# Streaming encoder step on one core: edges of order between prepared work and recurrence work on VectorE, ScalarE and GpSimd

## The chip, the cores and the metric

The kernel runs on one NeuronCore of a Trainium2 chip. The metric is the device time of one execution, in microseconds; of several executions the median is given.

## The reference

One layer of a hybrid streaming encoder over a prompt of 2048 positions and eight sample sequences of 16 positions each, all in float32, model width 1024:

```python
h = rms_norm(x, norm_mix)
p = h @ w_in                      # 3880 columns: q, k, v, z, gates of GDN; r, k, v, decay, gates of RWKV-7
x = x + concat(GDN(p_gdn), RWKV7(p_rwkv)) @ w_out
up = rms_norm(x, norm_ffn) @ w_up # 2 x 2816 columns
x = x + (silu(conv3(up[:, :2816])) * up[:, 2816:]) @ w_down
y = rms_norm(x, norm_final)
```

GDN is a gated delta rule with four heads of 128; RWKV-7 has eight heads of 64. Both carry a state from position to position. The q, k, v columns pass a short causal convolution of width 4, the RWKV columns one of width 2, the gate of the FFN one of width 3. Outputs are y and the final states of both request groups.

## The kernel before, in words

**Groups and phases.** The 16 blocks of 128 prompt positions are cut into five groups of 3, 4, 3, 3, 3 blocks; the last group carries the 128 sample positions too. A group's tiles are 128 channels by 384 or 512 positions. Each group has an input phase (`phase_in`, L551) and an output phase (`phase_out`, L1182). Their order is in0, in1, in2, out0, in3, out1, in4, out2, out3, out4 (`order`, L1293).

**Projections.** A product in float32 is made of three products of split operands: hi times hi, hi times lo, lo times hi (`mm3`, L447). A weight tile is split by `split_w` (L433): ScalarE casts the high part (L439), and VectorE or GpSimd in turn subtract it (L443). An activation tile is split by `split_x` (L507): ScalarE makes the high part (L512 or L515), VectorE the low part (L513 or L516). A phase splits its eight tiles of x first and then runs the blocks of columns, each into one of four PSUM banks. In an input phase the squares of x are summed beside the splits (`sumsq`, L477, L484). In an output phase the splits of `og` come first, then after `w_out` the splits of the new residual `res`.

**Prepared work.** The results of a column block are evicted, convolved (`conv`, L520: the history copy L526 on GpSimd, the eviction L527 on VectorE, the last tap L529 on ScalarE, the other taps L531 on VectorE), gated and stored to DRAM for the recurrences (`prep_gdn`, `prep_rwkv`, `l2scale`). In an output phase the same helpers make the FFN's gate, and L1241 adds a product in PSUM to the residual.

**Recurrence work.** `gdn_block` (L859) and `rwkv_half` (L1016) load a block's prepared tensors, build a 128 by 128 triangular system, invert it by seven doubling levels (`inverse`, L796: product pR, mask L821, product pX, addition L839), and advance the state. They run as tasks between the pieces of a later group's projection. Their many small steps go back and forth between TensorE and VectorE, ScalarE and GpSimd.

**Order of the work.** Everything is emitted by Python generators. `drive` (L391) holds a planner's clock of TensorE time (`mm` adds the cost of each product) and steps whichever task is due. Tasks have a rank: the projections, their prepared work and the norms have 0, the tails of the recurrences 1, RWKV 2, GDN 3. All that one step of a generator emits stands together. TensorE executes in the order of emission (`manual_schedule` names its engine, L1272). The order on VectorE, ScalarE, GpSimd and SP is set at compile time by the scheduler of the language, which takes, on its own estimate of time, the operations that are ready, so an operation emitted later may stand ahead of one emitted sooner on the same engine. Each engine then executes its list in order. All DMAs are issued from SP. Two places tie an operation behind the last one emitted on VectorE by hand (`behind`, L428, used at L653 and L781).

## Time and profile before

| | |
|---|---|
| median of three executions | 3531.19 us (3529.71 to 3534.89) |
| the profiled execution | 3535.21 us |
| its span, first to last instruction | 3533.4 us |
| mean granted clock of TensorE | 0.978 |
| TensorE busy with products | 3355.5 us (95%) |
| VectorE, GpSimd, ScalarE busy | 2371.1, 1843.7, 1512.1 us |

A row of a group or of the timeline gives the line, the engine (PE is TensorE, PEld its weight loads, DVE VectorE, ACT ScalarE, POOL GpSimd, SP the DMA queue), the operation, and what it writes and reads by the program's names. A row of waits says which engine's line waited for which other: total us, times, longest. A square bracket in the timeline gives the idle time of the engine before the operation and what ended it. Times are in us from the start of the span.

### The profile page before, as it was taken

Reading aid. Unit: us, or ns where it says so; the run is one execution under the profiler, and the core shown is the slowest. Engines: PE = TensorE matmul, PEld = TensorE weight load, DVE = VectorE, ACT = ScalarE, POOL = GpSimd, SP = SyncE. Lnnn points to the kernel's source line nnn. Section 1 sums busy time; section 2 is a strip of 40 time slices with the busy share of each in tenths; the row PEclk is TensorE's granted clock in tenths of the full one; section 3 lists DMA queues with packets and bytes.
Section 4 is the critical chain, followed back from the end, with each engine's and each line's share of the span. In section 5 each row is a group of like instructions: output and inputs, shape, how many; then the busy total and the mean of one; then the engine's idle time right before and its main releaser. Section 6 shows DMA issues by size and latency. Waiting matters only on the chain. (4 is left out here: it accounts for less than half of the span.)

```text
span 3533.4 us, 60005 instructions
## 1 busy us (share of the span) xinstructions
PE 3355.5 (95%) x21661; PEld 2888.1 (82%) x21661; DVE 2371.1 (67%) x4277; ACT 1512.1 (43%) x2698; POOL 1843.7 (52%) x2335
## 2 busy tenths in 40 slices
PE   8979989999999989999999999899999999999997
PEld 7857778889999878778877667699988899988886
DVE  6777777787666776766565777676657665665444
ACT  5554444444333454443333545443333444453333
POOL 4546556556666545556444445466656355534442
PEclk9989999999999999999999999999999999999999
DMA  5544444453333444533233334533334533443332
GB/s 170 170 127 135 144 151 126 131 174 113 115 114 105 123 145 148 173 93 91 90 93 90 121 120 144 186 116 113 114 119 153 164 120 126 138 143 96 96 94 82
DMA packets 346265, 447.58 MB, mean 127 GB/s; under 512 B 30168, under 2 KB 194336, under 8 KB 345968
## 3 DMA queue, kind: packets, MB, share of 16 engines
q1 hardware_dynamic: 345968, 443.75, 40.5%
q8 instruction: 170, 2.79, 0.3%
q14 instruction: 127, 1.04, 0.1%
HBM read 372.60 MB, written 71.03 MB: 126 GB/s over the span
## 5 line engine op out<-in xcount | busy, mean ns | idle before, releaser
L439 ACT CAST whi<-w 128x512 fp32r<-128x512 f32 (+1 forms) x1070 | 651.4, 610 | 1101.9 <-PE psd L362 282.8
L443 POOL TENSOR_TENSOR wlo<-w,whi 128x512 fp32r<-128x512 f32 (+1 forms) x535 | 705.0, 1318 | 721.9 <-ACT whi L439 695.1
L362 PE MATMUL psi<-x,whi 128*128 128x384 f32 (+1 forms) x2480 | 730.9, 376 | 34.5 <-ACT x L515 16.1
L362 PEld LDWEIGHTS psi<-x,whi 128*128 128x128 f32 x2480 | 454.1, 194 | 96.1 <-issue 21.6
L362 PE MATMUL psga<-x,whi 128*128 128x384 f32 (+1 forms) x1760 | 502.4, 366 | 0.0
L362 PE MATMUL psup<-x,whi 128*128 128x384 f32 (+1 forms) x1760 | 497.1, 363 | 0.0
L443 DVE TENSOR_TENSOR wlo<-w,whi 128x512 fp32r<-128x512 f32 (+1 forms) x535 | 428.2, 800 | 79.5 <-ACT whi L439 78.9
L362 PE MATMUL psi<-x,wlo 128*128 128x384 f32 (+1 forms) x1240 | 453.7, 366 | 4.3 <-POOL wlo L443 4.1
L362 PEld LDWEIGHTS psga<-x,whi 128*128 128x128 f32 x1760 | 318.5, 190 | 28.8 <-issue 3.6
L362 PEld LDWEIGHTS psup<-x,whi 128*128 128x128 f32 x1760 | 315.6, 188 | 26.6 <-issue 1.8
L362 PE MATMUL psd<-ah,whi 128*128 128x384 f32 (+1 forms) x880 | 328.1, 373 | 5.8 <-ACT ah L1231 5.8
L362 PE MATMUL psd<-al,whi 128*128 128x384 f32 (+1 forms) x880 | 318.8, 362 | 5.0 <-POOL al L1233 5.0
L362 PE MATMUL psd<-ah,wlo 128*128 128x384 f32 (+1 forms) x880 | 318.5, 362 | 0.0
L362 PE MATMUL psga<-x,wlo 128*128 128x384 f32 (+1 forms) x880 | 316.3, 359 | 0.0
L362 PE MATMUL psup<-x,wlo 128*128 128x384 f32 (+1 forms) x880 | 314.5, 357 | 0.0
L1241 DVE TENSOR_TENSOR res<-res,psd 128x384 f32<-128x384 f32 (+1 forms) x240 | 145.3, 606 | 201.3 <-PE psd L362 200.2
L362 PEld LDWEIGHTS psi<-x,wlo 128*128 128x128 f32 x1240 | 240.0, 194 | 28.0 <-POOL wlo L443 7.1
L1233 POOL TENSOR_TENSOR al<-xin,ah 128x384 fp32r<-128x384 f32 (+1 forms) x110 | 125.9, 1145 | 143.8 <-ACT ah L1231 103.1
L839 DVE TENSOR_TENSOR TUr<-TUr,pX 128x256 f16<-128x256 f16 x396 | 149.1, 413 | 73.4 <-PE pX L362 72.1
L527 DVE TENSOR_TENSOR P<-psga,rsx 128x384 f32<-128x384 f32 (+1 forms) x110 | 64.3, 585 | 192.9 <-PE psga L362 186.9
L362 PE MATMUL pso<-x,whi 128*128 128x384 f32 (+1 forms) x640 | 185.5, 370 | 2.1 <-DVE x L513 0.9
L362 PEld LDWEIGHTS psd<-ah,whi 128*128 128x128 f32 x880 | 166.6, 189 | 22.0 <-ACT ah L1231 7.2
(342 smaller groups left out, 6759.6 us busy)
## 6 DMA issues: line engine op xcount, KB each, us to landing
w<-in_w_up SPq DMA_DIRECT2D x440, 256.0 KB, 2.7
w<-in_w_in SPq DMA_DIRECT2D x310, 256.0 KB, 2.7
w<-in_w_down SPq DMA_DIRECT2D x160, 256.0 KB, 2.7
rX<-rx SPq DMA_DIRECT2D x68, 320.0 KB, 4.4
w<-in_w_out SPq DMA_DIRECT2D x80, 256.0 KB, 3.0
w<-in_w_down SPq DMA_DIRECT2D x80, 192.0 KB, 2.4
rx<-res SPq DMA_DIRECT2D x48, 192.0 KB, 3.0
gd<-res SPq DMA_DIRECT2D x48, 192.0 KB, 2.8
```

Of the source, the lines that this page charges most:

```text
L362: self.nc.tensor.matmul(out, lhsT=lhsT, rhs=rhs, start=start, stop=stop)
L439: nc.scalar.copy(hi, w)
L443: eng.tensor_tensor(lo, w, hi.bitcast(F32), SUB)
L527: nc.vector.tensor_tensor(P[:, h:h + g.P], ps[:, 0:g.P], rs[:, 0:g.P], MUL)
L839: nc.vector.tensor_tensor(w, w, pX[:, y].rearrange("p u (n b) -> p u n b", b=b), ADD)
L1233: nc.gpsimd.tensor_tensor(lo, y, hi.bitcast(F32), SUB)
L1241: nc.vector.tensor_tensor(res[m], res[m], ps, ADD)
```

## The change

The engines that the build writes to are wrapped. Each operation that is emitted on VectorE, ScalarE or GpSimd inside a step of a task with rank above 0 becomes that engine's mark. Each operation that is emitted outside such a step, and not inside `split_w`, gets an edge of order (no semaphore) to the mark of its own engine, so the scheduler may not put it ahead of it. Recurrence operations get no edge among themselves and none to prepared work; the splits of weights get none either. No instruction is added or removed, and the computation is the same.

```diff
+class Engine:
+    def __init__(self, b, eng):
+        self.b, self.eng, self.mark = b, eng, None
+
+    def __getattr__(self, op):
+        f = getattr(self.eng, op)
+
+        def run(*a, **k):
+            i = f(*a, **k)
+            if self.b.inrec:
+                self.mark = i.ins
+            elif self.mark is not None and not self.b.splitting:
+                self.b.tc.add_manual_dep(i.ins, self.mark.name, mybir.DependencyInfo(mybir.DependencyClass.NoSync, mybir.DependencyReason.DATA), reason="behind the recurrences")
+            return i
+        return run
+
+class Chip:
+    def __init__(self, b, nc):
+        self.nc = nc
+        self.vector, self.scalar, self.gpsimd = (Engine(b, e) for e in (nc.vector, nc.scalar, nc.gpsimd))
+
+    def __getattr__(self, name):
+        return getattr(self.nc, name)
...
-        self.tc, self.nc, self.I, self.O = tc, tc.nc, I, O
+        self.tc, self.nc, self.I, self.O = tc, Chip(self, tc.nc), I, O
+        self.inrec, self.splitting = False, False
...
     def step(self, task):
+        self.inrec = task[1] > 0
...
         out = []
+        self.splitting = True
         for w in ws or self.load_w(src, tiles):
...
             out.append((hi, lo))
+        self.splitting = False
         return out
```

## The prediction, made before the changed kernel was run

> **What bounds the kernel now.** I read the page first: its span, the busy line and the row of the GpSimd halves of the weights' splits.

> ```profile
> span 3533.4 us, 60005 instructions
> PE 3355.5 (95%) x21661; PEld 2888.1 (82%) x21661; DVE 2371.1 (67%) x4277; ACT 1512.1 (43%) x2698; POOL 1843.7 (52%) x2335
> L443 POOL TENSOR_TENSOR wlo<-w,whi 128x512 fp32r<-128x512 f32 (+1 forms) x535 | 705.0, 1318 | 721.9 <-ACT whi L439 695.1
> ```

> TensorE is the bound: 3533.4 - 3355.5 = 177.9 us of it are idle, and its order is written out, so an edge on another engine can only change how long it idles and how it is clocked. The change touches what VectorE, ScalarE and GpSimd run next, so the second view is who TensorE waits for.

> ```profile
> PE pA L362 <- DVE rA L1045: 18.2, 9, 4.5
> PE psi L362 <- ACT x L515: 16.1, 5, 7.1
> PE pR L362 <- DVE TUr L839: 12.3, 6, 5.6
> PE pX L362 <- DVE Rr L821: 8.1, 9, 2.5
> PE pSs L362 <- DVE gwm L988: 7.3, 4, 4.9
> ...
> PE pA L362 <- ACT rtok L1050: 6.0, 3, 2.3
> ...
> PE psi L362 <- DVE x L516: 5.3, 9, 1.6
> ...
> PE ptr L372 <- DVE TUg L839: 0.2, 1, 0.2
> ```

> Columns: total us, times, longest. The rows of this view whose releaser is a recurrence's tile (rA, TU, R, gwm, U, rtok and the like) are 25; the first and the last of them stand here, and they add up to 91.0 us, 2.6% of the span. That is all that shorter recurrence waits could ever return, apart from the clock.

> The third view, the timeline of VectorE at such waits, says what the late operation stood behind. Three kinds:

> ```profile
> 237.73 4.50 DVE L531 SCALAR_TENSOR_TENSOR res<-P,par,res 128x512 f32<-128x512 f32 x2
> 242.15 0.41 DVE L821 TENSOR_TENSOR Rr<-pR,msk 128x256 f16<-128x256 f32 x1
> 242.62 0.28 PE L362 MATMUL pX<-Rr,TUr 128*128 128x64 f16 x4 [1.37 <-DVE Rr L821]
> 1367.87 0.43 DVE L713 TENSOR_SCALAR lx<-lx 128x384 f32<-128x384 f32 x1 [1.15 <-POOL lx L712]
> 1368.33 0.96 DVE L714 TENSOR_TENSOR_SCAN ls<-scm,lx 128x387 f32<-128x387 f16 x1
> 1369.21 0.67 DVE L1045 TENSOR_TENSOR rA<-pA,msk 128x512 f32<-128x512 f32 x1
> 2284.10 0.69 DVE L443 TENSOR_TENSOR wlo<-w,whi 128x512 fp32r<-128x512 f32 x1 [1.89 <-ACT whi L439]
> 2284.70 1.28 DVE L1045 TENSOR_TENSOR rA<-pA,msk 128x512 f32<-128x512 f32 x2
> ```

> At 242 the mask `Rr` ran after two convolution taps of a column block that the code emits after it: this is what the change forbids. At 1368 `rA` stood behind decay work (L713, L714) that the code emits before `rA`: no edge touches that. At 2284 `rA` stood behind a split of weights, which the change sets aside. The longest single waits for `rA` and `gwm` in the rows above (4.5 and 4.9 us) are of the last two kinds or of the recurrence's own chain.

> **The change, part by part.** *What moves.* An edge ties each prepared operation to the last recurrence operation emitted on its engine (its mark), no more. I laid the order in which the code of before emits its operations beside the order in which the trace executes them. On VectorE 262 of 2052 prepared operations run before their mark, on ScalarE 85 of 1130, on GpSimd 146 of 972. Only these 493 are moved. 119 of GpSimd's are the tiny history copies of L526, which run long before their convolution, so their delay is hidden by that slack; I cost them at nothing (if the slack is gone, a copy is 0.4 us in front of a tap).

> *What it can return.* I followed each recurrence wait of TensorE back along its engine while that engine had no idle time. In 22 of the 70 that exceed 0.15 us a moved operation stands in this backlog; capping each by the smaller of wait and moved work gives 15.7 us. The first of the 22 is the one at 242, the last is this:

> ```profile
> 2802.61 0.70 PE L362 MATMUL pA<-rX 64*128 64x256 f32 x4 [2.31 <-ACT rtok L1050]
> 701.67 1.14 PE L362 MATMUL pKK<-gkq 128*128 128x256 f32 x2 [1.76 <-ACT gE L884]
> core 0: us, PE busy (x) PEld busy (x) DVE busy (x) ACT busy (x) POOL busy (x), PEclk, DMA share, GB/s
> 701.80:705.20 3.40, 3.40 (x9) 2.50 (x10) 0.00 (x0) 1.27 (x4) 3.40 (x4) 0.50 0.01 4
> ```

> The last two rows price the clock: a wait of 1.76 us is followed by 3.4 us at a granted clock of 0.50, which loses about half of 3.4, 1.7 us. Five of the 22 places (242 to 245, 1511 to 1513, 2029, 2570 to 2572, 2802) are followed by such a stretch: 5 x 1.7 = 8.5. So the most that can come back is 15.7 + 8.5 = 24.2 us. I take 60%, 14.5: a prepared operation that steps aside returns at once behind the mark and is in front of the next recurrence step.

> [...]

> *What it takes.* At the start of a projection the splits of x (L512 to L516) are emitted behind the recurrence step then open, and today they run ahead of it. Busy time of the VectorE splits alone, in the stretch that ends with the first product that reads them:

> ```profile
> 754.00:760.10 6.10, 2.42 (x5) 1.00 0.91 287
> 1211.00:1231.50 20.50, 4.33 (x5) 0.92 0.45 135
> 1985.00:2006.10 21.10, 4.61 (x5) 0.92 0.35 110
> 2726.00:2749.50 23.50, 5.30 (x8) 1.00 0.60 183
> 2749.34 0.74 DVE L839 TENSOR_TENSOR TUr<-TUr,pX 128x256 f16<-128x256 f16 x2
> 2749.49 0.51 PE L362 MATMUL pso<-x,whi 128*128 128x384 f32 x2
> 2750.02 0.51 PE L362 MATMUL pso<-x,whi 128*128 128x384 f32 x2
> L513 DVE TENSOR_TENSOR x<-x x40: 543/558/1501, 754.5 to 3093.7; 128x384 fp32r<-128x384 f32 x24, 128x512 fp32r<-128x512 f32 x16
> L516 DVE SCALAR_TENSOR_TENSOR x<-x,par x40: 605/712/1777, 7.1 to 2014.4; 128x384 fp32r<-128x384 f32 x24, 128x512 fp32r<-128x512 f32 x16
> L516 DVE SCALAR_TENSOR_TENSOR x<-res,par,x x40: 602/677/1784, 780.6 to 3150.7; 128x384 fp32r<-128x384 f32 x24, 128x512 fp32r<-128x512 f32 x16
> L484 DVE TENSOR_TENSOR rsx<-rsx,xin 128x384 f32<-128x384 f32 (+1 forms) x70 | 48.3, 690 | 4.3 <-ACT xin L483 3.5
> ```

> (Counts in brackets; in the L513 and L516 rows ns are least/median/most.) At 2749 all eight splits had run before the first product. Their mark there is the `TUr` that ends at 2749.34 + 0.74 = 2750.08. Behind it, tile 7 is ready at 2750.08 + 8 x 0.56 = 2754.6; the products, at 0.53 us a tile, want it at 2749.49 + 7 x 0.53 = 2753.2: 1.4 us lost, where today nothing waits. Output projections with recurrences still open start three times: 4.2. An input projection splits and sums squares, 0.71 + 0.69 = 1.40 a tile: 8 x 1.40 - 7 x 0.53 = 7.5, three times: 22.5. The splits of `res` ahead of the FFN: 8 x 0.68 - 7 x 0.53 = 1.7, four times: 6.9. Upper end 33.6. The lower end is near 3: marks that end before the first product, sums left for later, and splits that keep pace within 0.1 us a tile. I take half, 16.8: with the moved work gone from in front of it the mark itself ends sooner, and input projections wait for their splits already (5.3 us in the waits' row). Seven of these starts would lose 1.7 us or more, each then good for a slow stretch of the clock: 7 x 1.7 = 12, half of it 6.

> *Queues.* The edges bind no DMA, but a store waits for its operation on SP, and behind it stand the loads of weights:

> ```profile
> SPq L424 <- POOL wlo L443: 1155.1, 446, 9.1
> ...
> SPq L548 <- POOL res L730: 53.7, 43, 3.2
> ```

> Loads already wait for a split buffer nearly always; a store waits at most 3.2 us for `res`. Later by the moved operations' median of 2.6 us it would hold SP for some 6 us, less than the 8 us of products that four loaded weight tiles feed (16 tiles of 0.53 us). I cost it at nothing; without that cover it costs the difference. A moved `res + psd` (L1241, 49 of the 262) holds a PSUM bank longer; three other banks cover 6 us of products (12 tiles), and only four such moves are longer than that.

> *Sum.* Lost 16.8 + 6 = 22.8, returned 14.5: 8.3 us slower. The profiled execution took 3535.2 us with its span of 3533.4, 4.0 above the median of 3531.2; on the median the forecast is 3531.2 + 8.3, about **3540 us**. Some 0.2%, 7 us, is what a measurement of this kernel can tell from no change.

> **The rivals.**

> *The stalls go and the starts stay covered (not slower).* The recurrence work is ready sooner all along, so marks end before the first products, and the start loss stays at 3. Decisive is whether the mark ends before the first product that needs a split. For: 15.7 us of waits with moved work right in front; VectorE idles 33%, so delayed work has room. Against: `TUr` at 2749 ended 0.6 us after the product had begun. 24.2 - 3 gives up to 21 us; I put it at 18 faster, 3513. [...]

> *It evens out, or hardly changes the order.* One edge to the last mark leaves earlier recurrence operations free; 8732 of 9225 operations already stand as demanded. For: median displacement of 2.6 us on VectorE, and 75 of the 91 us lie in waits with no moved work in front, or beyond the cap. Time 3531, give or take 5.

> *Moved work meets GpSimd.* Of the x splits on VectorE 53 are moved into stretches where GpSimd splits weights back to back (1.32 us each). The L516 row shows 0.61 at least and 1.78 at most for one shape's work. Were each moved split to go from the median to the longest, 53 x (1.78 - 0.71) = 57 us would come on; with a third of that, 19, the time is 3559. Against: most x splits run near the median among the same weight splits today. [...]

> **How the numbers follow.** Forecast 0.44 (0.33 slower, 0.11 within the bound); stalls go 0.25 (0.23 faster, 0.02 same); evens out 0.20 (0.03 faster, 0.16 same, 0.01 slower); GpSimd 0.11 (slower). Together faster 0.26, same 0.29, slower 0.45. The range runs from a little beyond the faster case, 3510, to the GpSimd case, 3560; about 1 in 10 is left on either side. The forecast's own range is 3532 to 3553.

> **What would show it.** Right: the two rows for `psi` waiting on x (16.1 and 5.3 us) grow to 30 or more together, and `pso` gets rows of some us; no x split runs before its mark; the `Rr` at 242 follows its product at once; recurrence waits fall from 91 to about 75; rows like 1368 and 2284 stay. Wrong: recurrence waits halve, or the x rows stay as they are, or many slow-clock stretches go; GpSimd's case would show as L516 medians near 1 us. If `P` (L527) waits lengthen and `psi` waits for banks, my costing of the moved evictions at nothing failed.

## The result, and the profile after

| | before | after |
|---|---|---|
| median (4 executions each) | 3531.63 us (3529.71 to 3534.89) | 3567.04 us (3560.12 to 3575.9) |
| ratio | 1 | **1.0102, 95% interval 1.0088 to 1.0116** |
| span of the profiled execution | 3533.4 us | 3558.3 us |
| TensorE busy, idle | 3355.5, 177.9 us | 3361.9, 196.4 us |
| mean granted clock of TensorE | 0.978 | 0.975 |

The change makes the kernel 35 us slower. First the page of after, its span and its busy line.

```profile
span 3558.3 us, 59974 instructions
PE 3361.9 (94%) x21661; PEld 2888.3 (81%) x21661; DVE 2383.6 (67%) x4277; ACT 1513.3 (43%) x2698; POOL 1840.1 (52%) x2335
```

The same 21661 products run. TensorE idles 18.5 us more, and its products take 6.4 us more: together the 24.9 us by which the span grew. The profiled execution is the fastest of the four of after. The granted clock of the four was 0.972 to 0.976; in nine executions of before that ran beside the first experiments it was 0.977 to 0.980. Mean against mean (0.9748 and 0.9786) this is, as an estimate, 0.0038 x 3550 = 13.5 us. So of the 35 us some 18 are waits, as the one profiled execution shows them, and by this estimate some 14 are clock.

TensorE runs its 21661 products in the same order in both kernels, so they can be matched one by one. After is 8.4 us behind at 2500 us of before, 10.8 at 2700 and 25.1 at 2900: more than half of the growth falls into these 200 us, in which the prediction's start at 2749 lies.

Who TensorE waits for in after (columns as in the prediction: total us, times, longest). The wrapper gives every operation of the other three engines one line, L217; the tiles tell them apart.

```profile
PE pA L391 <- DVE rA L217: 18.3, 12, 4.6
PE psi L391 <- ACT x L217: 13.6, 3, 7.2
PE psi L391 <- DVE x L217: 12.9, 15, 2.6
PE pR L391 <- DVE TUr L217: 10.5, 6, 5.6
PE pSs L391 <- DVE gwm L217: 7.8, 4, 4.8
PE psd L391 <- ACT ah L217: 7.3, 5, 2.4
...
PE pso L391 <- DVE x L217: 6.9, 7, 3.5
...
PE psga L391 <- DVE x L217: 4.1, 4, 2.2
PE pk L401 <- issue: 3.9, 2, 2.1
```

Three sums of this view carry the comparison. All rows together rise from 158.6 to 177.1 us. The rows that wait for a split of x rise from 22.7 to 39.7: `psi` from 21.4 to 26.5, `pso` from 1.3 to 8.0 and `psga` from nothing to 5.2. The rows that wait for a recurrence's tile fall only from 91.0 to 84.3. What is left, prepared work, loads and splits of weights, rises from 44.9 to 53.1.

A view that the prediction does not use is VectorE's own waits. Of before, then of after:

```profile
DVE res L1241 <- PE psd L362: 200.2, 168, 3.3
DVE TUr L839 <- PE pX L362: 72.1, 61, 6.8
DVE Rr L821 <- PE pR L362: 69.9, 71, 4.2
DVE P L527 <- PE psi L362: 43.7, 33, 5.1
```

```profile
DVE res L217 <- PE psd L391: 155.9, 129, 3.7
DVE Rr L217 <- PE pR L391: 131.6, 101, 4.1
DVE TUr L217 <- PE pX L391: 96.8, 77, 5.1
DVE P L217 <- PE psi L391: 7.2, 10, 3.7
```

VectorE waits almost twice as long with `Rr` at the head of its list (69.9 to 131.6 us) and longer with `TUr` (72.1 to 96.8), and less with an eviction there (`P` of `psi` 43.7 to 7.2, `res` 200.2 to 155.9). Where an eviction used to wait for TensorE at the head of the list, a recurrence operation does now, and the eviction stands behind it. Summed over VectorE's instructions by what the code emits (each one's idle time before it), its idle time ahead of recurrence operations rose from 331 to 458 us, ahead of prepared work it fell from 729 to 587. VectorE's whole idle time hardly changes (1159 and 1172 us): it is the prepared operations behind a waiting head that come later.

The prediction's first place, 242 us of before, in the timeline of after (column in the bracket: idle before, and what ended it):

```profile
229.24 0.28 PE L391 MATMUL pR<-TUr,Nhr 128*128 128x64 f16 x4
229.63 0.43 DVE L217 TENSOR_TENSOR Rr<-pR,msk 128x256 f16<-128x256 f32 x1 [2.52 <-PE pR L391]
229.97 0.68 DVE L217 TENSOR_TENSOR P<-psi,rsx 128x512 f32<-128x512 f32 x1
...
232.20 0.29 PE L391 MATMUL pX<-Rr,TUr 128*128 128x64 f16 x4
```

`Rr` follows its product at once and `pX` waits for nothing: the 1.37 us of before are gone, and the 1.77 us behind them too. The stretch from 189 to 260 us is 11 us shorter; 5.5 of these come from 220 to 230 us, where a wait for `rA` is shorter (2.90 us in before, 1.32 in after) and a stretch at a granted clock of 0.50 (223.92 to 230.75 us of before) is gone. The price stands in the same rows: VectorE stood idle for 2.52 us with `P` behind `Rr`, though the last product of `P`'s bank had ended at 225.02.

One of the new waits for x, at 1452 us of after:

```profile
1445.41 0.69 DVE L217 TENSOR_TENSOR x<-x 128x512 fp32r<-128x512 f32 x1 [0.87 <-ACT x L217]
...
1451.18 0.56 DVE L217 SCALAR_TENSOR_TENSOR res<-res 128x384 f32<-128x384 f32 x1 [3.44 <-DMA res<-l]
1451.66 0.69 DVE L217 TENSOR_TENSOR x<-x 128x512 fp32r<-128x512 f32 x1
...
1452.40 0.80 PE L391 MATMUL pso<-x,whi 128*128 128x512 f32 x1 [3.48 <-DVE x L217]
```

In before these splits ran ahead of the tail of the recurrence. Moved behind it, one of them also stands behind a scaling by `l2scale` that waits 3.44 us for a load, and TensorE waits 3.48 us for the split. Such a start loses more than the splits' own time, which is all that the prediction counted.

### The profile page after: what moved, and what is told of

It reads as the page before. It is cut to its first block, busy times and chain, and to the rows that moved or that the text cites. A ratio compares the mean times of both kernels' runs of the same rounds, so it can differ in the third digit from the quotient of the medians.

```text
span 3558.3 us, 59974 instructions
## 1 busy us (share of the span) xinstructions
PE 3361.9 (94%) x21661; PEld 2888.3 (81%) x21661; DVE 2383.6 (67%) x4277; ACT 1513.3 (43%) x2698; POOL 1840.1 (52%) x2335
## 5 line engine op out<-in xcount | busy, mean ns | idle before, releaser
L217 POOL TENSOR_TENSOR wlo<-w,whi 128x512 fp32r<-128x512 f32 (+1 forms) x535 | 710.7, 1329 | 757.9 <-ACT whi L217 722.5
L217 ACT CAST whi<-w 128x512 fp32r<-128x512 f32 (+1 forms) x1070 | 652.2, 611 | 1050.7 <-PE psd L391 283.9
L217 DVE TENSOR_TENSOR wlo<-w,whi 128x512 fp32r<-128x512 f32 (+1 forms) x535 | 432.2, 808 | 109.3 <-ACT whi L217 108.8
L391 PEld LDWEIGHTS psup<-x,whi 128*128 128x128 f32 x1760 | 317.3, 189 | 26.5 <-issue 1.8
L217 DVE TENSOR_TENSOR res<-res,psd 128x384 f32<-128x384 f32 (+1 forms) x240 | 144.8, 605 | 156.7 <-PE psd L391 155.9
L217 DVE TENSOR_TENSOR TUr<-TUr,pX 128x256 f16<-128x256 f16 x396 | 149.4, 417 | 97.5 <-PE pX L391 96.8
L217 POOL TENSOR_TENSOR al<-xin,ah 128x384 fp32r<-128x384 f32 (+1 forms) x110 | 125.2, 1138 | 132.6 <-ACT ah L217 96.7
L217 DVE TENSOR_TENSOR Rr<-pR,msk 128x256 f16<-128x256 f32 x232 | 98.4, 424 | 133.8 <-PE pR L391 131.6
```

Of the source, the lines that this page charges most:

```text
L217: i = f(*a, **k)
L391: self.nc.tensor.matmul(out, lhsT=lhsT, rhs=rhs, start=start, stop=stop)
```

## The experiments

All variants add the change's edges to the kernel before in another place, after each step, so that lines stay apart (they lie some 30 further: `Rr` of L821 is L854, the eviction L527 is L560). A kind is noted for the operations of `split_w` ("w"), `split_x` ("x"), `sumsq` ("s") and, where used, VectorE's evictions of a projection's bank ("p"): the first operation of `conv` and its short one for the samples, z in `prep_gdn`, the two additions to the residual and the FFN's product.

```python
def tie(self, first, rec):            # after a step that emitted from `first` on
    for n in range(first, len(ins)):
        i, e = ins[n], engine(ins[n])
        if e not in ENGINES: continue
        if rec: self.mark[e] = i
        elif e in self.mark and self.bound(n, e): edge(i, self.mark[e])

def bound(self, n, e):
    return self.kinds.get(n, "") != "w"
```

The results: ratio to the kernel before on the same chip, and from the profiled execution the idle and busy time of TensorE and its waits for x, for `ah` and `al`, and for recurrence tiles, in us.

| run | edges | ratio [95%] | idle | busy | x | ah, al | rec. |
|---|---|---|---|---|---|---|---|
| before | none | 1 | 177.9 | 3355.5 | 22.7 | 10.8 | 91.0 |
| e0_same | the change | 1.0121 [1.0106, 1.0136] | 202.5 | 3370.9 | 40.9 | 12.6 | 86.8 |
| e1_rest | without x, s | 1.0087 [1.0071, 1.0102] | 192.5 | 3358.2 | 22.9 | 16.7 | 90.6 |
| e2_starts | x, s alone | 1.0037 [1.0024, 1.0050] | 184.5 | 3357.0 | 43.2 | 9.3 | 81.8 |
| e3_vector | VectorE | 1.0101 [1.0086, 1.0116] | 206.7 | 3355.4 | 32.8 | 12.6 | 92.5 |
| e4_act_pool | ScalarE, GpSimd | 1.0060 [1.0046, 1.0074] | 187.8 | 3365.8 | 34.1 | 12.2 | 85.9 |
| f1_pool | GpSimd | 1.0020 [1.0012, 1.0029] | 185.1 | 3355.9 | 19.0 | 15.1 | 93.7 |
| f2_act | ScalarE | 1.0007 [0.9998, 1.0017] | 177.9 | 3361.7 | 33.3 | 10.5 | 82.5 |
| e5_evict | p alone | 1.0079 [1.0066, 1.0092] | 196.5 | 3362.7 | 22.7 | 17.0 | 94.6 |
| g1_evict_in | p, input phases | 1.0039 [1.0026, 1.0053] | 189.6 | 3358.2 | 22.5 | 10.8 | 97.4 |
| g2_evict_out | p, output phases | 1.0038 [1.0025, 1.0051] | 188.0 | 3359.4 | 21.1 | 16.9 | 93.2 |
| e6_no_evict | without x, s, p | 1.0036 [1.0022, 1.0049] | 185.6 | 3361.8 | 22.4 | 14.9 | 90.1 |
| f3_taps | the same, VectorE | 0.9990 [0.9981, 0.9998] | 178.6 | 3354.1 | 22.2 | 10.6 | 89.9 |
| e7_aged | e1, mark 1.5 us old | 0.9995 [0.9987, 1.0004] | 175.3 | 3355.3 | 22.0 | 10.5 | 88.0 |
| f4_aged_all | e0, mark 1.5 us old | 1.0033 [1.0021, 1.0045] | 196.6 | 3349.3 | 29.2 | 9.0 | 88.6 |
| g3_evict_aged | p, mark 1.5 us old | **0.9965 [0.9952, 0.9979]** | 177.5 | 3348.3 | 22.2 | 10.8 | 88.4 |
| h1_evict_aged_07 | p, 0.7 us | 0.9996 [0.9987, 1.0005] | 179.7 | 3349.2 | 22.9 | 10.8 | 88.1 |
| h2_evict_aged_25 | p, 2.5 us | 0.9984 [0.9974, 0.9994] | 171.4 | 3358.2 | 22.8 | 10.8 | 88.2 |
| g4_taps_aged | f3 and g3 | 0.9994 [0.9985, 1.0003] | 183.1 | 3345.8 | 21.3 | 10.6 | 91.0 |

**Starts or the rest?** The first theory was the prediction's: the loss sits at the starts, in the splits of x.

```diff
# e1_rest
-    return self.kinds.get(n, "") != "w"
+    return self.kinds.get(n, "") not in ("w", "x", "s")
# e2_starts
+    return self.kinds.get(n, "") in ("x", "s")
# e3_vector: the rule of e0_same with
+ENGINES = ("DVE",)
```

> The change itself, written so that the line numbers of its operations stay apart (the edges are added after each step and not in a wrapper; the order on every engine is that of the changed kernel, 3567 us). All theories: 1.008 to 1.012 of the kernel before. If it comes out under 1.005, part of the 35 us belonged to that measurement and not to the change.

> Edges on everything but the splits of x (split_x) and the sums of squares (sumsq), splits of weights aside as before. Theory of the starts: the loss sits in the splits of x behind a late mark at the starts of projections (17 us of waits) and the slow stretches they bring (8 us or more), so without these edges the loss is gone and the shorter recurrence waits stay: 3520 to 3533 us, x waits of TensorE back near 16 us. Rival of the rest: the moved evictions, taps and stores hold banks, SP and with it the loads of weights and of gkq, and the 8 us of other waits plus most of the clock's loss are theirs: 3548 us or more, with x waits near 16 us all the same. Rival of mere order: any changed order costs about this much, whatever is tied: 3545 to 3570.

> Edges on the splits of x and the sums of squares alone. Theory of the starts: nearly the whole loss is there, 3552 to 3567 us, x waits of 30 us or more, recurrence waits within 5 us of the 91 before. Rival of the rest: 3535 to 3548 us, since only the 17 us of x waits less what later waits give back remain. Rival of mere order: like the other part, 3545 to 3570, and the two parts' losses together are more than the whole change's 35 us.

> Edges as in the change, but on VectorE alone. 262 of the 493 moved operations and all low parts of x are there. Theory of the starts: most of the loss stays, 3555 to 3567 us. If instead the high parts on ScalarE or GpSimd's copies and sums, tied behind their own marks, set the starts: 3530 to 3545.

The theory of the starts falls. Without any edge on x, a loss of 0.87% stays, with the waits for x as in before (22.9 us); with those edges alone it is 0.37%, though they bring the whole of the x waits (43.2 us): 9 us come back in shorter recurrence waits. VectorE's edges alone cost as much as the change. e0_same repeats the result and shows the clock's part: its order is that of after, its waits are 182.6 against 177.1 us, and its products take 9.0 us longer at a clock of 0.974.

**Which of the rest?** The second theory, of the heads: a tied operation puts a recurrence operation that still waits for its product at the head of VectorE's list.

```diff
# e4_act_pool
+ENGINES = ("Activation", "Pool")
# e5_evict
+    return self.kinds.get(n, "") == "p"
# e6_no_evict
+    return self.kinds.get(n, "") not in ("w", "x", "s", "p")
# e7_aged: marks are kept with the planner's clock at their emission; the edge goes
# to the newest one with clock <= now - 1500 ns, and x, s, w get none
+        elif (m := self.old(e)) is not None and self.bound(n, e): edge(i, m)
```

> Edges on ScalarE and GpSimd alone, all prepared work but the splits of weights. VectorE alone gave 1.0101 of the kernel before. Theory of the heads (a tied operation on VectorE puts a recurrence operation that still waits for its product at the head of VectorE's list, and VectorE stands idle): nothing of that here, 3524 to 3538 us. Rival, that moved work costs wherever it is moved: 85 + 146 of the 493 moved operations are here, a third to a half of the loss, 3542 to 3550 us.

> Edges only on VectorE's evictions of the projections' PSUM banks (the first operation of conv, its short one for the samples, the gate's z, the residual's two additions, the FFN's product): 151 of VectorE's 262 moved operations. Theory of the heads: they are emitted 0.2 to 0.4 us of products after a mark whose product is still in flight, so they carry most of the rest's loss, 3548 to 3562 us, and VectorE's wait for pR before Rr rises from 70 us to 110 or more. Rival of the late chains (taps, gates and squares pushed back, and with them stores, SP and loads): 3530 to 3542 us. Rival of the banks: as the heads in time, but then waits of TensorE for P and for banks carry it and not VectorE's idle time.

> Edges on all three engines, but not on splits of x, sums of squares or evictions of PSUM: taps, gates, norms and copies alone. Theory of the heads: the taps stand behind their own eviction, which runs free again, so VectorE is rarely held; 3524 to 3537 us. Rival of the late chains: the loss of the rest stays here, 3545 us or more. Both: the Rr at 242 us of the kernel before no longer stands behind taps.

> Edges as in the first part alone (no splits of x, no sums, on three engines), but to the newest mark that is at least 1.5 us of the planner's clock old when the operation is emitted. Theory of the heads: the product of such a mark is back by then, VectorE is not held, and the loss goes; what the change returned near 242 us may stay: 3520 to 3535 us, VectorE's wait for pR near 70 us. Rival of mere order (any change of the scheduler's order costs, 111 operations of VectorE stand elsewhere here): 3540 us or more.

The evictions alone, 151 of the 493 moved operations, cost 0.79%, and VectorE's waits in that run are those of the whole change:

```profile
DVE Rr L854 <- PE pR L364: 140.9, 97, 5.4
DVE TUr L872 <- PE pX L364: 99.5, 76, 5.1
```

Banks are a small part: of TensorE's waits for a bank not yet freed, `res` is a new row of 3.0 us, and that of `psi` for `P` (7.1 before) is 6.8. All of TensorE's rows rise from 158.6 to 177.4 us. The largest part, 6.2 us, is `ah` and `al`, what hangs on the eviction; recurrence tiles take 3.6, `res` 3.0, the rest are small rows of gates and sums. The last product of the FFN's upward half before `w_down`, in before (VectorE, ScalarE, TensorE) and in e5_evict:

```profile
2729.97 0.54 DVE L1229 TENSOR_TENSOR xin<-xin,psup 128x384 f32<-128x384 f32 x1
2730.55 0.52 ACT L1231 CAST ah<-xin 128x384 fp32r<-128x384 f32 x1 [0.25 <-DVE xin L1229]
2731.12 0.44 PE L362 MATMUL psd<-ah,whi 128*128 128x384 f32 x1
```

```profile
2748.27 0.68 DVE L1078 TENSOR_TENSOR rA<-pA,msk 128x512 f32<-128x512 f32 x1
2748.87 0.41 DVE L1180 TENSOR_TENSOR rot<-ptr,rrh 128x256 f32<-128x256 f32 x1
2749.20 0.54 DVE L1262 TENSOR_TENSOR xin<-xin,psup 128x384 f32<-128x384 f32 x1
2749.77 0.51 ACT L1264 CAST ah<-xin 128x384 fp32r<-128x384 f32 x1 [0.17 <-DVE xin L1262]
2750.34 0.44 PE L364 MATMUL psd<-ah,whi 128*128 128x384 f32 x1 [3.24 <-ACT ah L1264]
2753.14 0.69 PE L364 MATMUL psd<-al,whi 128*128 128x384 f32 x1 [2.36 <-POOL al L1266]
```

In before the FFN's product ran ahead of the last two `rA` and of `rot`. Tied behind `rot`, it comes last, the splits `ah` and `al` after it, and TensorE waits 3.24 us and then 2.36 us (before: nothing and 0.80). This is a start too, of `w_down`, that the prediction did not count. VectorE is not idle in these rows: here the product is late by the work that it was put behind, not by a head that waits.

e7_aged removes the whole 0.87% with 1.5 us of age (VectorE's wait for pR is back at 85.0 us). Half of VectorE's moved operations were emitted within 0.43 us of products after their mark, and these are no longer bound by it. The traces show how many stay moved: 160 of VectorE's 704 evictions stand behind more recurrence operations than in before in e1_rest, and 32 in e7_aged. So the age does not only change what a moved eviction stands behind; most evictions no longer move at all.

Two runs missed what the heads forecast: e4_act_pool lost 0.60% and e6_no_evict 0.36% where nothing or little was expected. So something besides VectorE's heads and the splits of x costs, and the next runs look for it.

**ScalarE, GpSimd, taps, and the age for x.**

```diff
# f1_pool, f2_act: the rule of e0_same with one engine
+ENGINES = ("Pool",)          # f2_act: ("Activation",)
# f3_taps: ENGINES = ("DVE",) with the rule of e6_no_evict
# f4_aged_all: the age of e7_aged, with x and s bound too
```

> Edges on GpSimd alone: 146 moved operations, 119 of them the history copies in front of a convolution, which the prediction cost at nothing. Theory that the copies have slack: 3524 to 3536 us. Rival, that a late copy holds the eviction of its convolution and so a PSUM bank and the taps: 3540 us or more, the larger part of what ScalarE and GpSimd gave together (1.0060).

> Edges on ScalarE alone: 85 moved operations, 40 of them high parts of x. Theory that the starts carry what ScalarE and GpSimd gave together (1.0060): x waits of TensorE rise from 16 to 27 us or more, 3540 to 3552 us. Rival, that GpSimd carries it: 3536 us or less.

> Edges on VectorE alone, and there only on operations that are no splits of x, no sums and no evictions: taps, gates and norms, 46 moved operations. Theory of the heads (only a tied operation whose mark still waits for its product holds VectorE; taps stand behind their eviction anyway): 3522 to 3536 us, perhaps a gain of some us from the stalls near 242 us. Rival of the late chains: half or more of the 0.36% of the run without evictions, 3537 us or more.

> The whole change, splits of x and sums too, but each edge to the newest mark that is at least 1.5 us of the planner's clock old. Theory that young marks alone cost: 3525 to 3538 us, x waits near 16 us, VectorE's wait for pR near 80 us. Rival, that splits of x lose at the starts whatever the mark's age: x waits 28 us or more, 3542 us or more.

f3_taps is the theory's case without cost: taps follow their own eviction, and where that runs free, the edge returns a little (0.10%). f4_aged_all divides the two losses: with aged marks the rest loses nothing (e7_aged), and the edges on x and on the sums still cost 0.38% more. So at the starts it is not the young mark: in both e0_same and f4_aged_all 69 of VectorE's splits of x stand behind more recurrence operations than in before, so there the age does not undo the moves. TensorE's waits for x rise by 6.5 us there, and its product of the norm, `psn`, waits 13.7 us for a sum of squares (`acc`) instead of 3.2; what delays these sums was not traced further. GpSimd's edges, 119 of 146 on copies, cost 0.20%, part of the 0.36% that e6_no_evict had lost; the taps give -0.10%, and the rest of the 0.36% stays open. In f1_pool TensorE's waits for splits of weights and for `al`, which GpSimd makes too, rose from 10.5 to 16.7 us (5.5 + 5.0 to 8.6 + 8.1). ScalarE alone cannot be told from none: its x waits are 10.6 us longer (33.3) and its recurrence waits 8.5 us shorter. The two together gave 0.60% and apart 0.27%; half of the profiled difference of e4_act_pool is clock (busy 10.3 us more at 0.974), and why they add up to more than their sum stays open.

**Age alone, and the phases.**

```diff
# g1_evict_in, g2_evict_out: the rule of e5_evict and
+    ... and self.phase == "in"          # g2_evict_out: "out"
# g3_evict_aged, h1_evict_aged_07, h2_evict_aged_25: the rule of e5_evict with marks
# that are 1500, 700, 2500 ns old
# g4_taps_aged: VectorE alone; taps, gates and norms to the newest mark, "p" as in g3
```

> Edges on VectorE's evictions alone, and only while an input phase runs (69 of the 151 moved evictions are of psi, the rest of the output phases). Theory of the heads: each phase pays where recurrences are open beside it, so roughly half of 1.0079, 3543 to 3552 us if before is 3533, and VectorE's wait for pR near 105 us. Rival, that output phases alone pay (their splits of ah and al hang on the eviction of psup): 3538 us or less.

> The same while an output phase runs. Theory of the heads: the other half, 3543 to 3552 us, with TensorE's waits for ah and al at 15 us or more where they were 10.8. Rival, that input phases alone pay (evictions there stand in front of convolutions and the recurrences' own gE on ScalarE): 3538 us or less.

> Edges on VectorE's evictions alone, to the newest mark that is at least 1.5 us of the planner's clock old. Theory of the heads: nothing is lost, 0.998 to 1.002 of the kernel before, VectorE idle before recurrence operations some 30 us above the 331 and not 130. Rival, that tied evictions lose whatever the age (as splits of x do): 1.004 or more.

> VectorE alone: taps, gates and norms tied to the newest mark (0.9990 alone), evictions to the newest mark at least 1.5 us old, splits of x and sums free. Theory of the heads: both lose nothing and the gains near 242 us stay, 0.997 to 1.000 of the kernel before. If edges lose by their number, 1.002 or more.

> Edges on VectorE's evictions alone, to the newest mark at least 0.7 us of the planner's clock old (a product of an inverse takes 0.3 us, and half of the moved operations were emitted 0.4 us or less after their mark). Theory of the heads: the marks in flight are left out already, 0.996 to 1.001 of the kernel before. If a mark needs more than a round trip of 1 to 2 us to be harmless: 1.002 or more, VectorE's wait for pR above 95 us.

> The same with 2.5 us. Theory of the heads: fewer edges that matter, so a smaller gain or none, 0.996 to 1.001. If the gain of the 1.5 us edge was one lucky order, either run may come out at 1.002 or more.

The evictions' loss divides into equal halves, 0.39% and 0.38%, and `ah` and `al` belong to the output half (16.9 us), as expected. VectorE's wait for pR rises mostly there, to 121.3 us; in the input half it is 90.4, below the 105 expected, though the time is lost all the same. The age alone turns 1.0079 into 0.9965. VectorE's waits of g3_evict_aged:

```profile
DVE Rr L860 <- PE pR L364: 81.8, 69, 5.3
DVE TUr L878 <- PE pX L364: 74.6, 60, 6.8
```

But of the evictions 159 stand later than in before in e5_evict, and only 31 in g3_evict_aged (40 at 0.7 us of age, 23 at 2.5). So the loss goes with the moves that the young marks forced, and the 31 that stay cost nothing that can be seen. Whether a move is harmless because its mark's product is back is not shown: that would need the same evictions moved behind old marks and behind young ones. g3_evict_aged is faster than both kernels, 3521.74 us against 3534.15. Its gain is not what the edges are for: TensorE idles as in before (177.5 us), and its products take 7.2 us less, at a clock of 0.980 (the profiled execution is the slowest of its five). At 0.7 and 2.5 us of age the ratio is 0.9996 and 0.9984, and with the taps' edges added (g4_taps_aged) 0.9994. That the loss is gone holds for all three ages; the size of the gain hangs on the order that comes out, and why that order is granted more clock was not settled.

## Why the prediction was wrong

Its sign was right, its size was not: 8 us forecast, 35 measured, beyond the range's end of 3560 us.

**The step that failed** is the one under *Queues* that costs moved evictions at nothing: a moved `res + psd` "holds a PSUM bank longer; three other banks cover 6 us of products (12 tiles)". The other evictions were not costed at all. By themselves the edges on evictions cost 0.79%, 28 us (e5_evict). The cover that I named, three banks, was there (one bank wait of 3.0 us). But a bank is only the first thing that hangs on an eviction. Convolution, gate, `ah` and `al` hang on it too, and on VectorE, which executes its list in order (in after `P` stood 2.52 us behind the waiting `Rr` at 229 us), all that is queued behind the mark hangs on the mark's product. The prediction said where moved work goes ("returns at once behind the mark") and did not ask what VectorE does until the mark is ready: it waits with `Rr` at its head, 62 us more, and an eviction that could run stands behind. How much of the 28 us is this wait and how much the mere later place in the list (as at 2749 us of e5_evict) stays open.

The sign that the prediction named for this failure did not come: `P` was to wait longer and `psi` to wait for banks. VectorE's wait with `P` of `psi` at its head fell to 7.2 us, and TensorE's wait of `psi` for `P` stayed (7.1 and 6.6). It looked for the failure at the bank, where little happened.

**The gain** was mis-sized. I took 14.5 us of 24.2. The wait at 242 us went as described, but the recurrence rows fell by 6.7 us in all, to 84.3 and not to about 75: the likely reason, not shown place by place, is the prediction's own, that work kept out from in front of one recurrence step is in front of the next. From 260 to 475 us after takes back 14.7 us, more than the 11 that it had gained before.

**The starts** came out at the right sum, by luck, and were placed partly wrong: the waits for x rose by 17.0 us where I had taken 16.8. The rows of `psi` grew by 5.1 us, to 26.5 and not to 30 or more; those of `pso` grew by 6.7, beyond the 4.2 that I had as their upper end, and those of `psga`, the FFN's start, by 5.2. Their net cost is smaller, 0.37% or 13 us, since recurrence waits fall in exchange (e2_starts).

**The history copies** of GpSimd were costed at nothing. All of GpSimd's edges cost 0.20%, 7 us (f1_pool).

**The clock** was priced at 6 lost and 8.5 regained, of which I counted 60%. By the estimate above it cost some 14 us: waits did not go, they moved and became more.

The parts do not add up: x alone 0.37%, evictions 0.79% and the others 0.36% are 1.5% against 1.0 to 1.2% of the whole. That TensorE has two late inputs at the same place and pays once would explain it, but is not shown.

**The rivals.** "The stalls go" and "it evens out" are refuted by the ratio. "Moved work meets GpSimd" came nearest in time, 3559 us, by a mechanism that did not happen. The splits of x in e0_same:

```profile
L548 DVE SCALAR_TENSOR_TENSOR x<-x,par x40: 603/634/1789, 7.1 to 2028.7; 128x384 fp32r<-128x384 f32 x24, 128x512 fp32r<-128x512 f32 x16
L548 DVE SCALAR_TENSOR_TENSOR x<-res,par,x x40: 602/744/1677, 830.1 to 3190.9; 128x384 fp32r<-128x384 f32 x24, 128x512 fp32r<-128x512 f32 x16
```

Their medians, 0.63 and 0.74 us, are close to those of before (0.71 and 0.68), not near 1 us. VectorE's busy time as a whole grew by 12.5 us (2371.1 to 2383.6); in which operations was not traced.

## What to carry to other kernels

An edge "B behind A" on an engine that executes its list in order, as VectorE does in these traces, can cost what A still waits for and what else stands in front of it, paid by B and by all that is queued behind B: before adding it, look up in that engine's own waits how long A stands at the head, and what needs B next. Tying to an older mark (here 0.7 to 2.5 us) took the evictions' loss away, mostly by leaving four of five evictions where they were; count what an edge really moves. And price a delayed operation by everything that hangs on it (the start of the next projection), not by the buffer that it frees.
